# A mixture-of-experts layer on one core: slot rows and row fetches one stage later, the accumulator's writes issued from ScalarE, the residual joined in the last rounds

## The chip, the core and the metric

The kernel runs on one core of one Trainium2 chip. The metric is device time of one execution in microseconds. Three runs of the kernel before gave 2064.96, 2068.54 and 2069.97 us; the median, 2068.54, is the time to compare with. All engine names are those of the profile: PE is TensorE's matmul stream, PEld its weight loads, DVE is VectorE, ACT is ScalarE, POOL is GpSimd, SP is SyncE.

## The reference

One layer over 512 latent tokens of width 1024. A token mixer with two branches (a bidirectional RWKV scan and a gating MLP) comes first; the change does not touch it. Then comes this part, which it does touch:

```python
h = modulate(rmsnorm(x, norm2_g[l]), sh2, sc2)
x = x + ga2 * moe_ffn(h, lp)
...
return rmsnorm(x, final_norm_g)
```

`moe_ffn` sends every token to 4 of 32 experts. With `xblk` the rows of one expert's tokens, an expert computes

```python
gate = xblk @ lp['exp_w_gate'][e] + lp['exp_b_gate'][e]
up = xblk @ lp['exp_w_up'][e] + lp['exp_b_up'][e]
return clamped_swiglu(gate, up) @ lp['exp_w_down'][e] + lp['exp_b_down'][e]
```

and the results are added back to the tokens with softmax weights. All matrices are 1024 by 1024 in fp32, so the 32 experts read 96 of them, 4 MB each.

## The kernel before, in words

The part before the experts (projections, scan, merge, router) takes the first 834 us. The experts take the rest. They are written out by hand in `expert_chain` (from L1642): for PE, ACT and DVE the order of the program is the order of execution, while the DMA orders of SP and POOL are set by a scheduler.

**Rounds and places.** Round r has twelve places: 0 to 3 are the four weight blocks of the gate matrix of expert r, 4 to 7 the four blocks of the down matrix of expert r-1, 8 to 11 the four blocks of the up matrix of expert r. Round 0 has no down blocks, round 32 only down blocks. A weight block is 1 MB: SP loads it into a `raw` tile (six buffers), ACT casts it to fp32r (`wh`, L1481, called three blocks ahead), DVE forms the remainder (`wl`, L1487, two blocks ahead), and PE multiplies (L1498, L1499, L1503). A `raw` buffer is free again when the `wl` of its block is done.

**Between the blocks.** The activation of expert r-1 stands in round r: `up_clamp` and `up_half` on DVE at places 1 and 2, the transposes of `turn` on PE (L1583, followed by ACT's `aH`, L1586, and DVE's `aL`, L1587) after places 2 and 4. `x_rows` (L1534) lets POOL fetch the token rows of an expert by their slot numbers from DRAM; `x_turn` (L1547) transposes them after places 6 and 8. `y_out` scales an expert's output and lets POOL add it into the accumulator `d_acc` in DRAM.

**The side work.** `side` is a generator of which one piece is emitted per place, from round 0 on: `sum_start` forms the gate-weighted bias of the down projection on PE, copies it with ACT into a tile (L1425) and writes it to `d_acc` as the accumulator's start value (L1426 and L1429, five writes from SP, through one buffer, so that each pair of copies waits for the write before). Then `slot_rows` makes the slot numbers (L1379 to L1390) from a table that POOL scattered to DRAM and read back (`places`, L1368 and L1372), then `counts` (L1313 to L1322, with four small matmuls, L1318), `beyond` (L1438 to L1447) and `last_table` (L1752 to L1758).

**The end.** Experts 30 and 31 do not go through the accumulator: PE multiplies their outputs with a one-hot table. `x_load` and `sum_load`, emitted at the start of round 31, bring back the residual x, the final norm's weights, the gate `ga2` and the accumulator; `x_sum` (L1785, L1786) adds gate times accumulator to x on DVE, once for each of the four token tiles. `last_part(i, j)` (L1798, L1799) joins x of tile i and the expert output j in PSUM: j = 0 is expert 30, j = 1 is expert 31. The four tiles use PSUM tiles `gp`, `up`, `gp`, `up` in turn. `finish` then squares a tile on ACT (L1815), takes the root (L1816), scales on DVE (L1821), writes the output from SP (L1822), and copies the tile's sum back to x (L1823).

Of the kernel before, what the change touches and what calls it, by code (L numbers as in the profile page):

```python
# [154 lines left out]
class K:  # L155
# [1154 lines left out]
    def counts(self, pool):  # L1310
# [3 lines left out]
        pc = self.ps.tile([128, 32], F32, name="b1")  # L1314
# [9 lines left out]
    def places(self, pool):  # L1324
# [45 lines left out]
        self.tab = moe.tile([128, 4, NE, 2], F32, name="am")  # L1370
# [21 lines left out]
    def sum_start(self, pool):  # L1392
# [27 lines left out]
        for i in range(4):  # L1420
# [136 lines left out]
    def gate_sig(self, E):  # L1557
# [5 lines left out]
        nc.scalar.activation(sg, sg, AF.Sigmoid, scale=-1.702, bias=self.eps[:, 5:6])  # L1563

# [64 lines left out]
    def experts(self):  # L1629
        self.xf, self.xg, self.pss = [], {}, {}  # L1630
        self.nsplit = 0
# [15 lines left out]
    def expert_chain(self):  # L1647
# [31 lines left out]
        for i, (r, e, n, pos) in enumerate(seq):  # L1679
# [21 lines left out]
            elif pos == 4:  # L1701
                P["dn"] = ps.tile([128, 2, 512], F32, name="dn", bufs=1)
                if r == NE:
# [84 lines left out]
    def last_part(self, i, j):  # L1788

        nc = self.nc  # L1790
        if j == 0:
            self.pss[i] = self.ps.tile([128, 2, 512], F32, name=("gp", "up", "gp", "up")[i], bufs=1)
        ps = self.pss[i]
        y = self.ylast[j]
        for c in range(2):
            cs = slice(512 * c, 512 * c + 512)
            if j == 0:
                nc.tensor.matmul(ps[:, c, :], self.ident, self.xf[i][:, cs], start=True, stop=False)  # L1798
            nc.tensor.matmul(ps[:, c, :], self.wT[:, j, i, :], y[:, cs], start=False, stop=(j == 1))  # L1799

    def finish(self, P):

        nc = self.nc
        self.y_out(P)
        self.ylast[1] = P["y"]
        for i in range(4):
            if i > 1:
                self.last_part(i, 0)
            self.last_part(i, 1)
            x = self.xf[i]  # L1810
# [284 lines left out]
```

## Time and profile before

| what | value |
|---|---|
| median of three runs | 2068.54 us (2064.96 to 2069.97) |
| the profiled execution | 2063.39 us |
| its span, first to last instruction | 2061.6 us |
| PE busy | 1957.5 us (95%) |
| DVE busy | 1655.9 us (80%) |
| ACT busy | 1226.7 us (60%) |
| POOL busy | 422.9 us (21%) |
| mean granted clock of TensorE | 0.962 of full speed |

Busy shares are means over stages with different limits. Times on the timeline count from the span's start. In a timeline row the columns are start, duration, engine, line, operation, output and input, shape, how many, and in brackets the engine's idle time before the row with what ended it. A bracket that names an engine which had long been done hides another cause, often a DMA.

### The profile page before, as it was taken

What the parts mean: (1) busy time and instruction counts of PE and PEld (TensorE: products, weight loads), DVE (VectorE), ACT (ScalarE), POOL (GpSimd) and SP (SyncE); (2) the same over time, 40 slices, a digit from 0 to 9 for tenths busy, and PEclk for the clock granted to TensorE, in tenths of its full rate; (3) what the DMA queues carried; (4) which work ended last, traced back from release to release, by engine and by line L of the source; (5) the groups of instructions that cost most, each with busy time, mean ns of one, the idle gap of its engine ahead of it and who ended that gap; (6) DMA issues with size and microseconds to landing.
All of it is one profiled execution on the core that took longest, in us unless ns stands there. A gap on an engine that the chain in (4) does not pass through costs nothing.

```text
span 2061.6 us, 29221 instructions
## 1 busy us (share of the span) xinstructions
PE 1957.5 (95%) x11300; PEld 1524.1 (74%) x11300; DVE 1655.9 (80%) x1767; ACT 1226.7 (60%) x1387; POOL 422.9 (21%) x385
## 2 busy tenths in 40 slices
PE   7999889999999988889999999999999999999986
PEld 4667666666666678768888888888888888888863
DVE  5755875777766367789999999989999998999984
ACT  4522534343524244767777777777777777777752
POOL 0001605343423353510101011010101101010000
PEclk9999987988979998989999999999999999999999
DMA  8666232121112185789999999999999999999991
GB/s 312 212 204 196 61 118 78 40 64 32 51 42 69 33 270 215 278 288 377 364 373 368 371 369 367 375 364 379 369 371 368 365 374 367 375 366 374 366 357 43
DMA packets 153810, 534.26 MB, mean 259 GB/s; under 512 B 16160, under 2 KB 77344, under 8 KB 104513
## 3 DMA queue, kind: packets, MB, share of 16 engines
q1 hardware_dynamic: 141351, 500.57, 65.2%
q0 software_dynamic: 9952, 25.89, 5.2%
q10 hardware_dynamic: 2362, 5.87, 0.7%
q8 instruction: 91, 1.49, 0.3%
q14 instruction: 54, 0.44, 0.1%
HBM read 502.58 MB, written 37.65 MB: 262 GB/s over the span
## 4 chain that ended last, share of the span: by engine, by line
PE 72%; DVE 6%; issue 3%; POOL 3%; DMA 2%; ACT 1%; SPq 0%; POOLq 0%; DVEq 0%; ACTq 0%
PE dn L1499 6%; PE dn L1498 6%; PE dn L1503 6%; PE up L1498 6%; PE up L1499 6%; PE up L1503 6%; PE gp L1498 5%; PE gp L1499 5%; PE gp L1503 5%; PE fill L1082 4%; PE b L1583 1%; PE mm L868 1%; PE b L1547 1%; PE ch L909 1%; PE acc L165 1%
## 5 line engine op out<-in xcount | busy, mean ns | idle before, releaser
L1487 DVE TENSOR_TENSOR wl<-raw,wh 128x2048 fp32r<-128x2048 f32 x384 | 864.8, 2284 | 59.5 <-PE gp L1503 30.5
L1481 ACT CAST wh<-raw 128x2048 fp32r<-128x2048 f32 x384 | 721.5, 1905 | 104.9 <-PE gp L1499 68.3
L1498 PE MATMUL dn<-wh,aH 128*128 128x512 f32 x512 | 208.6, 407 | 6.5 <-ACT aH L1586 6.5
L1498 PE MATMUL gp<-wh,xH 128*128 128x512 f32 x512 | 206.4, 403 | 0.0
L1498 PE MATMUL up<-wh,xH 128*128 128x512 f32 x512 | 204.8, 400 | 0.0
L1499 PE MATMUL gp<-wh,xL 128*128 128x512 f32 x512 | 203.8, 398 | 0.0
L1499 PE MATMUL dn<-wh,aL 128*128 128x512 f32 x512 | 203.5, 397 | 0.0
L1534 POOL DMA_INDIRECT xg<-d_h,slots x30 | 33.9, 1129 | 824.4 <-PE b L1547 815.7
L1499 PE MATMUL up<-wh,xL 128*128 128x512 f32 x512 | 202.3, 395 | 0.0
L1503 PE MATMUL dn<-wl,aH 128*128 128x512 f32 x512 | 140.1, 395 | 0.0
L1503 PE MATMUL gp<-wl,xH 128*128 128x512 f32 x512 | 139.9, 395 | 0.0
L1503 PE MATMUL up<-wl,xH 128*128 128x512 f32 x512 | 139.3, 394 | 0.0
L1601 POOL DMA_INDIRECT d_acc<-y,slotd x30 | 105.0, 3501 | 132.4 <-ACT y L1600 99.7
L1586 ACT CAST aH<-b 128x512 fp32r<-128x512 f32 x64 | 37.6, 588 | 142.0 <-PE b L1583 142.0
L1498 PEld LDWEIGHTS dn<-wh,aH 128*128 128x128 f32 x512 | 97.1, 190 | 27.1 <-ACT aH L1586 7.0
L1503 PEld LDWEIGHTS gp<-wl,xH 128*128 128x128 f32 x512 | 96.6, 189 | 23.7
L1503 PEld LDWEIGHTS dn<-wl,aH 128*128 128x128 f32 x512 | 96.6, 189 | 22.3
L1499 PEld LDWEIGHTS gp<-wh,xL 128*128 128x128 f32 x512 | 97.0, 189 | 21.8
L1499 PEld LDWEIGHTS dn<-wh,aL 128*128 128x128 f32 x512 | 97.2, 190 | 21.3 <-DVE aL L1587 0.7
L1503 PEld LDWEIGHTS up<-wl,xH 128*128 128x128 f32 x512 | 96.1, 188 | 22.7
L1498 PEld LDWEIGHTS gp<-wh,xH 128*128 128x128 f32 x512 | 96.9, 189 | 21.6
L1498 PEld LDWEIGHTS up<-wh,xH 128*128 128x128 f32 x512 | 96.2, 188 | 22.2
(516 smaller groups left out, 3830.6 us busy)
## 6 DMA issues: line engine op xcount, KB each, us to landing
raw<-in_exp_w_gate_dram SPq DMA_DIRECT2D x128, 1024.0 KB, 7.0
raw<-in_exp_w_up_dram SPq DMA_DIRECT2D x128, 1024.0 KB, 9.2
raw<-in_exp_w_down_dram SPq DMA_DIRECT2D x128, 1024.0 KB, 7.1
raw<-in_w_ada_dram SPq DMA_DIRECT2D x32, 512.0 KB, 3.6
raw<-in_w_in_dram SPq DMA_DIRECT2D x24, 512.0 KB, 3.9
wa<-in_w_ada_dram SPq DMA_DIRECT2D x7, 1024.0 KB, 13.6
raw<-in_w_in_dram SPq DMA_DIRECT2D x6, 1024.0 KB
raw<-in_w_o_dram SPq DMA_DIRECT2D x8, 512.0 KB
```

What stands on the lines that cost most here:

```text
L165: return mm(ps, aH, bL, start=False, stop=last)
L868: nc.tensor.matmul(mm[:, par, d, :], BK[r, d, ch[d], :], AR[r, d, ch[d], :], start=True, stop=True)
L909: nc.tensor.matmul(sp[:, d, :], bk[:, d, :], uv[:, d, :], start=True, stop=True)
L1082: nc.tensor.matmul(ps, a[:, k, :], b[:, k, :], start=(n == 0), stop=(n == 23))
L1481: self.nc.scalar.copy(h, t)
L1487: self.nc.vector.tensor_sub(lo, t, h)
L1498: mm(ps[:, c, :], xH[:, k0 + kk, :], wh[:, cs], start=first and kk == 0, stop=False)
L1499: mm(ps[:, c, :], xL[:, k0 + kk, :], wh[:, cs], start=False, stop=False)
L1503: mm(ps[:, c, :], xH[:, k0 + kk, :], wl[:, cs], start=False, stop=last and kk == 1)
L1534: self.nc.gpsimd.indirect_dma_start(out=t, out_offset=None, in_=self.d_h2, in_offset=bass.IndirectOffsetOnAxis(ap=self.slots[:, e:e + 1], ...
L1586: nc.scalar.copy(aH, pt)
L1601: nc.gpsimd.indirect_dma_start(out=self.d_acc, out_offset=bass.IndirectOffsetOnAxis(ap=self.slotd[:, e:e + 1], axis=0), in_=y, in_offset=N ...
```

## The change

- **Round 1.** `counts` is split in two and comes right after `sum_start`. `slot_rows` waits until place 4 of round 1 is past (`rows_due`). The row fetches for experts 2 and 3 follow at places 4 and 5 instead of 3 and 5, and the transposes of expert 2's rows stand after places 8 and 10 instead of 6 and 8. The table read back from DRAM gets the buffer named `y` instead of `am`.
- **The accumulator's start value.** Its five writes are issued from ACT instead of SP.
- **The residual.** `x_sum(0)` stands at place 10 of round 31 instead of place 4; `x_sum` 1 to 3 stand at places 5 to 7 of round 32 (before: one at place 10 of round 31, two at places 6 and 7 of round 32).
- **The last four tiles.** Each has a PSUM tile of its own (`gp`, `up`, two `b1` tiles, `dn`). `last_part(1, 0)` moves from before the down blocks of expert 31 to behind them. The root's function table is asked for in round 31, behind the last sigmoid, and the four copies back to x stand at the very end, as eight halves.

```diff
+        yield
+        pc = self.ps.tile([128, 32], F32, name="b1")
         for j in range(4):
             nc.tensor.matmul(pc, self.ones, ch[:, j, :], start=(j == 0), stop=(j == 3))
...
-        self.tab = moe.tile([128, 4, NE, 2], F32, name="am")
+        self.tab = moe.tile([128, 4, NE, 2], F32, name="y")
...
-            nc.sync.dma_start(self.d_acc[128 * i:128 * i + 128, :], self.keep[:, 2048:3072])
+            nc.scalar.dma_start(self.d_acc[128 * i:128 * i + 128, :], self.keep[:, 2048:3072])
             yield
-        nc.sync.dma_start(self.d_acc[NLAT:NLAT + 128, :], self.keep[:, 2048:3072])
+        nc.scalar.dma_start(self.d_acc[NLAT:NLAT + 128, :], self.keep[:, 2048:3072])
...
+        if E["e"] == NE - 1:
+            nc.scalar.activation(self.moe.tile([128, 1], F32, name="rs", bufs=2), self.eps[:, 4:5], AF.Sqrt)
...
         yield from self.sum_start(self.small)
+        yield from self.counts(self.small)
+        yield
+        while not self.rows_due:
+            yield
         yield from self.slot_rows(self.small)
-        yield
-        self.counts(self.small)
         yield
         self.beyond(self.small)
...
-                    self.last_part(1, 0)
-                elif r == NE - 1:
-                    self.x_sum(0)
-            elif r == NE and pos > 5:
+            elif r == NE:
                 self.x_sum(pos - 4)
...
             elif pos == 10 and r == NE - 1:
-                self.x_sum(1)
+                self.x_sum(0)
...
-            elif pos in (6, 8) and r < NE and P:
-                self.x_turn(r + 1, pos // 2 - 3, xT)
+            elif pos in ((6, 8) if r > 1 else (8, 10)) and r < NE and P:
+                self.x_turn(r + 1, int(pos == (8 if r > 1 else 10)), xT)
+            if r == 1 and pos == 4:
+                self.rows_due = True
             next(side, None)
-            if r == 1 and pos in (3, 5):
-                self.x_rows(2 + (pos == 5))
+            if r == 1 and pos in (4, 5):
+                self.x_rows(pos - 2)
...
-            self.pss[i] = self.ps.tile([128, 2, 512], F32, name=("gp", "up", "gp", "up")[i], bufs=1)
+            if i < 3:
+                t = self.ps.tile([128, 2, 512], F32, name=("gp", "up", "dn")[i], bufs=1)
+                self.pss[i] = [t[:, 0, :], t[:, 1, :]], t.rearrange("p a b -> p (a b)")
+            else:
+                self.pss[i] = [self.ps.tile([128, 512], F32, name="b1") for _ in range(2)], None
...
+        self.last_part(1, 0)
         self.y_out(P)
         self.ylast[1] = P["y"]
-        for i in range(4):
-            if i > 1:
+        self.last_part(0, 1)
+        self.last_part(1, 1)
+        for n, i in enumerate((0, 1, 3, 2)):
+            if n > 1:
                 self.last_part(i, 0)
-            self.last_part(i, 1)
+                self.last_part(i, 1)
...
-            nc.scalar.copy(x, pf)
+        for i in (0, 1, 3, 2):
+            for c in range(2):
+                nc.scalar.copy(self.xf[i][:, 512 * c:512 * c + 512], self.pss[i][0][c])
```

The order on three engines follows. On DVE, the start of round 1, before: `slv` to `slots` are `slot_rows`, `sg` and the first `am` are the activation of expert 0.

```order
L1487 TENSOR_TENSOR wl<-raw,wh 128x2048 x2
L1379 TENSOR_REDUCE slv<-am 128x64
L1381 COPY wslot<-slv 128x32
L1383 TENSOR_SCALAR slm<-slv 128x32
L1385 SCALAR_TENSOR_TENSOR slots<-slm,slv 128x32
L1386 TENSOR_SCALAR slots<-slots 128x32
L1487 TENSOR_TENSOR wl<-raw,wh 128x2048
L1572 TENSOR_SCALAR sg<-up 128x1024
L1577 SCALAR_TENSOR_TENSOR am<-sg,gg 128x512
```

The same place in the changed kernel:

```order
L1315 TENSOR_SCALAR ch<-pm 128x128
L1488 TENSOR_TENSOR wl<-raw,wh 128x2048
L1576 TENSOR_SCALAR sg<-up 128x1024
L1581 SCALAR_TENSOR_TENSOR am<-sg,gg 128x512
L1321 TENSOR_REDUCE mc<-b_8532 128x1
L1323 CAST maxc<-mc 128x1
L1488 TENSOR_TENSOR wl<-raw,wh 128x2048
L1581 SCALAR_TENSOR_TENSOR am<-sg,gg 128x512
L1591 TENSOR_TENSOR aL<-b_8560,aH 128x512
L1488 TENSOR_TENSOR wl<-raw,wh 128x2048 x2
L1591 TENSOR_TENSOR aL<-b_8606,aH 128x512
L1380 TENSOR_REDUCE slv<-y 128x64
```

The slot rows moved from ahead of the activation to behind both of its halves and behind four more `wl`; the two steps of `counts` stand where they stood or close by.

On SP, rounds 0 and 1, before (`d_acc` are the accumulator's start writes):

```order
L1463 DMA raw<-in_exp_w_gate_dram 128x2048 x2
L1426 DMA d_acc<-mH 128x1024
L1463 DMA raw<-in_exp_w_gate_dram 128x2048
L1426 DMA d_acc<-mH 128x1024
L1463 DMA raw<-in_exp_w_gate_dram 128x2048
L1463 DMA raw<-in_exp_w_down_dram 128x2048
L1426 DMA d_acc<-mH 128x1024
L1463 DMA raw<-in_exp_w_down_dram 128x2048
L1426 DMA d_acc<-mH 128x1024
L1429 DMA d_acc<-mH 128x1024
L1463 DMA raw<-in_exp_w_down_dram 128x2048 x2
```

And now (the loads of `final_norm_g` and of `d_mod`, which is `ga2`, stood in round 31 before):

```order
L1464 DMA raw<-in_exp_w_gate_dram 128x2048 x4
L1464 DMA raw<-in_exp_w_down_dram 128x2048 x3
L1776 DMA mH<-in_final_norm_g_dram 128x1024
L1464 DMA raw<-in_exp_w_down_dram 128x2048
L1464 DMA raw<-in_exp_w_up_dram 128x2048
L1779 DMA mH<-d_mod 128x1024
L1464 DMA raw<-in_exp_w_up_dram 128x2048 x3
L1464 DMA raw<-in_exp_w_gate_dram 128x2048 x3
```

No weight load stands behind an accumulator write on SP any more, and two loads of 512 KB moved from round 31 to rounds 0 and 1.

On PE, the end of the program behind the last down block, before (`am` is the output of expert 31, `y` that of expert 30):

```order
L1799 MATMUL gp<-am,mH 128x512 x2
L1799 MATMUL up<-am,mH 128x512 x2
L1798 MATMUL gp<-xH,first 128x512
L1799 MATMUL gp<-y,mH 128x512
L1798 MATMUL gp<-xH,first 128x512
L1799 MATMUL gp<-y,mH 128x512
L1799 MATMUL gp<-am,mH 128x512 x2
```

And now:

```order
L1808 MATMUL up<-xL,first 128x512
L1809 MATMUL up<-y,mH 128x512
L1808 MATMUL up<-xL,first 128x512
L1809 MATMUL up<-y,mH 128x512
L1809 MATMUL gp<-am,mH 128x512 x2
L1809 MATMUL up<-am,mH 128x512 x2
L1808 MATMUL b_17150<-xL,first 128x512
L1809 MATMUL b_17150<-y,mH 128x512
```

The four matmuls of `last_part(1, 0)` now open this stretch, and the third tile goes to `b1` tiles instead of to `gp` again.

## Rows read from the trace of the kernel before

**Rows 1.** Stretches: round 1, then round 2 (busy, granted clock, DMA share, GB/s).
```profile
862.00:914.20 52.20, 39.28 (x171) 31.19 (x171) 38.82 (x43) 30.98 (x24) 12.99 (x9) 0.84 0.80 285
914.40:950.60 36.20, 36.20 (x166) 29.38 (x165) 33.77 (x21) 27.35 (x19) 4.62 (x3) 1.00 1.00 373
```

**Rows 2.** Timeline of PE in round 1: its two waits.
```profile
880.06 1.12 PE L1583 MATMUL b<-first,am 128*128 128x128 f32 x4 [9.46 <-DVE am L1577]
884.63 0.27 PE L1318 MATMUL b<-ch,ones 128*128 128x32 bf16 x4 [3.46 <-DVE ch L1316]
```

**Rows 3.** Timeline of DVE in round 1.
```profile
867.03 2.29 DVE L1487 TENSOR_TENSOR wl<-raw,wh 128x2048 fp32r<-128x2048 f32 x1 [4.50 <-ACT wh L1481]
874.22 0.58 DVE L1379 TENSOR_REDUCE slv<-am 128x64 f32<-128x256 f32 x1 [4.90 <-DMA am<-d_tab]
```

**Rows 4.** Timeline of ACT and its DMA issues, and of SP, rounds 0 and 1.
```profile
180.41 0.33 ACTq L552 DMA_DIRECT2D d_r<-ro  x1
...
848.02 0.33 SPq L1426 DMA_DIRECT2D d_acc<-mH  x1
...
851.09 1.08 ACT L1425 COPY mH<-b 128x512 f32<-128x512 f32 x2 [1.28 <-DMA d_acc<-mH]
...
858.43 0.33 SPq L1426 DMA_DIRECT2D d_acc<-mH  x1
...
864.12 1.07 ACT L1425 COPY mH<-b 128x512 f32<-128x512 f32 x2 [3.92 <-PE gp L1499]
```

**Rows 5.** DMA issues of the whole run: count, KB each, median us to landing.
```profile
d_acc<-mH SPq DMA_DIRECT2D x5, 512.0 KB, 3.8
...
d_v<-vo ACTq DMA_DIRECT2D x4, 384.0 KB, 4.8
...
d_r<-ro ACTq DMA_DIRECT2D x4, 256.0 KB, 2.0
...
d_acc<-y,slotd POOLq DMA_INDIRECT x30, 13.1
```

**Rows 6.** Waits of SP's queue, 830 to 900 us: total, times, longest.
```profile
SPq L1426 <- ACT mH L1425: 20.7, 4, 7.0
```

**Rows 7.** Timeline of POOL, round 1: the first row fetch.
```profile
876.34 2.37 POOL L1534 DMA_INDIRECT xg<-d_h,slots  x1 [8.33 <-DMA raw<-in_exp_w_down_dram]
```

**Rows 8.** Timeline of all engines in round 31, and the root's table load.
```profile
1965.82 0.49 SPq L1773 DMA_DIRECT2D mH<-d_mod  x1
...
1983.51 0.79 PE L1498 MATMUL dn<-wh,aH 128*128 128x512 f32 x1 [6.53 <-ACT aH L1586]
...
1988.95 1.22 DVE L1785 TENSOR_TENSOR raw<-raw,mH 128x1024 f32<-128x1024 f32 x1
...
1995.62 5.50 ACT L1481 CAST wh<-raw 128x2048 fp32r<-128x2048 f32 x3
1997.55 6.70 DVE L1487 TENSOR_TENSOR wl<-raw,wh 128x2048 fp32r<-128x2048 f32 x3
...
2037.89 1.28 ACT L1816 ACT_TABLE_LOAD   x1
```

**Rows 9.** Timeline of PE in round 32 and at the end.
```profile
2016.72 1.11 PE L1583 MATMUL b<-first,am 128*128 128x128 f32 x4 [3.52 <-DVE am L1577]
...
2021.79 0.79 PE L1498 MATMUL dn<-wh,aH 128*128 128x512 f32 x1
...
2034.74 1.98 PE L1799 MATMUL gp<-am,mH 128*128 128x512 f32 x4 [0.78 <-DVE am L1598]
...
2042.17 1.12 PE L1798 MATMUL gp<-xH,first 128*128 128x512 f32 x2 [3.74 <-ACT xH L1823]
```

**Rows 10.** Timeline of DVE in round 32.
```profile
2018.49 0.69 DVE L1587 TENSOR_TENSOR aL<-b,aH 128x512 fp32r<-128x512 f32 x1 [1.82 <-ACT aH L1586]
...
2026.23 0.69 DVE L1587 TENSOR_TENSOR aL<-b,aH 128x512 fp32r<-128x512 f32 x1 [6.07 <-ACT aH L1586]
...
2033.99 1.29 DVE L1598 TENSOR_TENSOR am<-dn,mH 128x512 f32<-128x512 f32 x2
```

More of the change, by code (lines that the diff above doesn't have):

```diff
@@ L1630, in experts @@
         self.xf, self.xg, self.pss = [], {}, {}
+        self.rows_due = False
         self.nsplit = 0
@@ L1796, in last_part @@
             cs = slice(512 * c, 512 * c + 512)
             if j == 0:
-                nc.tensor.matmul(ps[:, c, :], self.ident, self.xf[i][:, cs], start=True, stop=False)
-            nc.tensor.matmul(ps[:, c, :], self.wT[:, j, i, :], y[:, cs], start=False, stop=(j == 1))
+                nc.tensor.matmul(ps, self.ident, self.xf[i][:, cs], start=True, stop=False)
+            nc.tensor.matmul(ps, self.wT[:, j, i, :], y[:, cs], start=False, stop=(j == 1))
     def finish(self, P):
         nc = self.nc
+        self.last_part(1, 0)
@@ L1804, in finish @@
         self.y_out(P)
         self.ylast[1] = P["y"]
-        for i in range(4):
-            if i > 1:
+        self.last_part(0, 1)
+        self.last_part(1, 1)
+        for n, i in enumerate((0, 1, 3, 2)):
+            if n > 1:
                 self.last_part(i, 0)
-            self.last_part(i, 1)
-            x = self.xf[i]
+                self.last_part(i, 1)
+            parts, whole = self.pss[i]
             o = self.mbW.tile([128, 2048], F32, name="wh", bufs=4)[:, :1024]
-            pf = self.pss[i].rearrange("p a b -> p (a b)")
@@ L1813, in finish @@
             rs = self.moe.tile([128, 1], F32, name="rs", bufs=2)
-            ss = self.moe.tile([128, 1], F32, name="ss", bufs=2)
-            nc.scalar.activation(o, pf, AF.Square, accum_out=ss)
-            nc.scalar.activation(rs, ss, AF.Sqrt, bias=self.eps[:, 0:1], scale=1.0 / 1024)
-            nc.vector.reciprocal(rs, rs)
-            n = 1 + (i == 3)
-            for c in range(n):
-                cs = slice(1024 // n * c, 1024 // n * (c + 1))
-                nc.vector.scalar_tensor_tensor(o[:, cs], pf[:, cs], rs, self.fin[:, cs], op0=OP.mult, op1=OP.mult)
-                nc.sync.dma_start(self.out[128 * i:128 * i + 128, cs], o[:, cs])
@@ L1823, in finish @@
-            nc.scalar.copy(x, pf)
+            ss = self.moe.tile([128, 2], F32, name="ss", bufs=2)
+            if i < 3:
+                nc.scalar.activation(o, whole, AF.Square, accum_out=ss[:, 0:1])
+            else:
+                for c in range(2):
+                    nc.scalar.activation(o[:, 512 * c:512 * c + 512], parts[c], AF.Square, accum_out=ss[:, c:c + 1])
+                nc.vector.tensor_add(ss[:, 0:1], ss[:, 0:1], ss[:, 1:2])
+            nc.scalar.activation(rs, ss[:, 0:1], AF.Sqrt, bias=self.eps[:, 0:1], scale=1.0 / 1024)
@@ new lines, in finish @@
+            nc.vector.reciprocal(rs, rs)
+            for c in range(2):
+                cs = slice(512 * c, 512 * c + 512)
+                if n < 2:
+                    if c == 0:
+                        nc.vector.scalar_tensor_tensor(o, whole, rs, self.fin, op0=OP.mult, op1=OP.mult)
+                        nc.sync.dma_start(self.out[128 * i:128 * i + 128, :], o)
+                else:
+                    nc.vector.scalar_tensor_tensor(o[:, cs], parts[c], rs, self.fin[:, cs], op0=OP.mult, op1=OP.mult)
+                    nc.sync.dma_start(self.out[128 * i:128 * i + 128, cs], o[:, cs])
@@ L1825, in final_norm @@
+        for i in (0, 1, 3, 2):
+            for c in range(2):
+                nc.scalar.copy(self.xf[i][:, 512 * c:512 * c + 512], self.pss[i][0][c])
     def final_norm(self, i, pool, o, n=1):
```

3 lines of the change are left out of this document (1 added, 2 removed).

## The prediction

> **What bounds the kernel now.** I read the timeline by stretches first. In a steady round PE is busy for 36.20 of 36.20 us at full granted clock, with DVE at 33.77 us and the DMA engines at a share of 1.00 [rows 1]. So 29 of the 32 rounds belong to PE, DVE and DMA have little to spare, and the change touches nothing there. Round 1 is the exception: 52.20 us, of which PE works 39.28 at a mean clock of 0.84 and DVE 38.82 [rows 1]. Then I read who waits in it. PE stands still twice, 9.46 us for the activation of expert 0 and 3.46 us for the token counts, both from DVE [rows 2]. DVE stands still before that: 4.50 us for a cast of ACT, and 4.90 us at `slv` for the table that POOL reads back [rows 3]. DVE works in order, so the activation and three `wl` queue behind a table that PE does not need yet. At the other end two waits of PE matter: 6.53 us in round 31 for weights that come late [rows 8], and 3.74 us before the third token tile, whose PSUM tile ACT is still copying [rows 9].
>
> **Round 1: 7.7 us.** The slot rows move behind both halves of the activation and four `wl`. The table is read at 874.22 [rows 3]; behind the moved work (four `wl` of 2.29 us alone are 9.2 us) `slv` finds it ready, so that wait goes. What is late next is DVE itself: it has 38.82 us of work in 52.20 us [rows 1], thus 13.4 us of idle time. The first 4.50 us of it [rows 3] lie ahead of the slot rows and stay. The other 8.9 us follow from the slot rows or from PE's waits behind them, and go if DVE runs without a gap. PE needs less than that: its 39.28 busy us are partly at a low clock. So DVE, not PE, sets the length of the new round, and I expect short waits of PE for it at several places, the one-hot table of `last_table` among them.
>
> The new writes from ACT cost some of this, because the 4.50 us have a cause on ACT: it copies into one buffer and waits until each accumulator write has landed. The copy at 851.09 followed a write issued at 848.02, 3.1 us; the copy at 864.12 followed one issued at 858.43, 5.7 us [rows 4] (the bracket names PE, which was done long before). In the changed order ACT issues four of the five writes ahead of the cast that DVE waits for: 4 x 0.33 us by an earlier issue from ACT [rows 4], 1.3 us more. The landing of such a write from ACT is not in the trace. Its nearest rows are 3.8 us for these same writes from SP and 4.8 us for 384 KB from ACT [rows 5]; I take 4.3. The first wait then grows by 1.2 us and the last shrinks by 1.4, so DVE starts 1.1 to 1.2 us later: 8.9 - 1.2 = 7.7 us.
>
> Against this the Trainium skill's page "DMA: Bandwidth & Descriptors", section "Queues, rings and completion order", says that each DMA engine takes turns between the queues that have work, packet by packet. By that rule a write on ACT's own queue does not stand behind the megabytes of weights on SP's; with the lower row, 3.8 us, the first wait grows by 0.7, the last shrinks by 1.9, the round would gain 8.8 and the whole 12.7 us. No row here shows two busy queues with such a write, so I stay between the two rows.
>
> SP, freed of waiting 20.7 us for ACT's copies [rows 6], issues weight loads earlier; I give that no time of its own, since ACT did not wait for weights in this round. The two 512 KB loads that now stand in rounds 0 and 1 do not bind: 52.20 us at 285 GB/s are 14.9 MB, with 1.05 MB more 15.9 MB, which at the steady 373 GB/s [rows 1] take 42.7 us, below the 44.5 us that remain. The second of them waits on SP for the accumulator's last write; the weight loads behind it belong to places 9 to 11, and have some 10 us of slack. The split `counts` asks its matmuls one block earlier; what they then wait for is the same chain on DVE. The ends for the round: 13.4 us if all idle time of DVE goes, and less than nothing if the writes land late (below).
>
> **Round 31: 0.8 us.** The `ga2` load of 512 KB leaves SP's queue just ahead of the late weights [rows 8]. Alone on the engines it takes 1.4 us at 373 GB/s; beside the accumulator's read-back, which POOL issues at that time, up to twice that. I take 2.1 us off PE's wait of 6.53 us. But ACT now loads the root's table behind the sigmoid of this round: 1.28 us [rows 8], ahead of the three casts from 1995.62, and DVE's `wl` from 1997.55 starts the moment the first of these is done [rows 8]. From there DVE runs without a gap into PE's 3.52 us wait of round 32 [rows 9], so the load is paid: 2.1 - 1.3 = 0.8. Taking `x_sum(0)` out of place 4 frees 2.4 us of DVE (two operations of 1.22 [rows 8]) ahead of that point, where ACT is the later one, so I count nothing for it. Ends: -1.3 if the DMA gains nothing, 4 if the table load is covered and part of those 2.4 us counts.
>
> **Round 32 and the end: 3.1 us.** `last_part(1, 0)` leaves the stretch between PE's transposes, which end at 2017.83, and the down blocks, which start at 2021.79 [rows 9]: 3.96 us. The down blocks can now start when `aL` is done, at 2019.18 [rows 10], 2.6 us earlier, and end near 2031.4 instead of 2033.96. The second `aL` then ends at 2024.3 instead of 2026.92 [rows 10]; behind it come one `wl` (2.29) and now three `x_sum` (six operations of 1.22, 7.3 us, against 4.9 before), so DVE is free for `y` at 2033.9. Before, it took `y` at 2033.99 [rows 10]. So expert 31's output is neither earlier nor later; what moves in front of it is covered by `last_part(1, 0)`, which ends at 2031.4 + 3.96 = 2035.3, against a start of the next part at 2034.74 [rows 9]: 0.6 us lost. Behind that the same matmuls follow as before, without the wait of 3.74 us [rows 9], for the third and fourth tile have PSUM of their own. 3.74 - 0.6 = 3.1 us. The chain behind the last matmul is the same; the eight copies now at the end run beside the output's DMA. Ends: 0.5 us if a low clock after PE's wait eats the 2.6 us, 4 if `last_part(1, 0)` runs faster than it did there.
>
> **The sum.** 7.7 + 0.8 + 3.1 = 11.6 us. The profiled execution took 2063.39 us, so 2051.8 in its terms; it lies 5 us below the median of 2068.54, which is what the next times are to be held against: 2068.54 - 11.6 = 2056.9 us. About 0.3%, 6.2 us, is what a measurement of this kernel can tell from no change: faster means below 2062.3.
>
> **The rivals.**
> - *ACT becomes the bound, slower.* Each pair of copies waits in ACT's order for the write before, and every cast behind it waits too. POOL's scattered adds of the same size land after 13.1 us [rows 5]. If ACT's writes took that under full DMA load, the two waits seen would grow by 10.0 and 7.4 us, the covered one between by about as much: some 26 us, against 8.9 gained. 8.9 - 26 + 3.9 = -13, 2082 us. It decides from a landing of about 9 us on. Against it: the five writes took 3.8 us even in SP's queue [rows 5]. Chance 0.05.
> - *The row fetch comes late.* The slots are ready near 885 instead of 875.5, so the fetch, issued at 876.34 before [rows 7], goes out near 886, while PE reaches the transposes (two blocks later in order) near 895. If it lands like POOL's adds, after 13.1 us, PE waits 4 us, and the round gains 3.7: 2060.9. For it: POOL is slow and the DMA full; against it: a fetch only reads. Chance 0.14.
> - *The writes land quickly.* With the 2.0 us of a 256 KB write from ACT [rows 5], the waits shrink by 1.1 and 3.7 while the issues cost 1.3: DVE restarts 3.5 us earlier, the round gains 12.4, the whole 16.3: 2052.2. Against it: 373 GB/s would stretch the round to 42.7 us again, about 2055. Chance 0.15.
> - *The order does not do what it says,* and the slot rows still hold DVE: only 3.9 us remain, 2064.6. The order on DVE speaks against it. Chance 0.04.
>
> **The numbers.** The forecast has 0.62, with its own range 2051 to 2062 from the ends above taken two at a time. The range is 2049 to 2063: it leaves out the slower rival, the fourth, and the far end of the third. Faster: nearly all of the forecast, the third rival and most of the second, 0.85; same 0.10; slower 0.05.
>
> **What would show it.** In the changed profile round 1 lasts 44 to 45 us between the first blocks of rounds 1 and 2, `slv` follows `aL` without waiting for a DMA, and DVE has no idle time over 1 us from the third `wl` of the round on. ACT's waits for `d_acc` are 3 to 5 us each. PE's wait in round 31 is 4 to 5 us, its wait at the last activation 3.5 to 5. The last tiles follow each other on PE without a gap. A wait of ACT for a write above 9 us, or of PE for `xg`, would make the forecast wrong; so would a PE clock that falls in the new round 1 and stays low.

## The result, and the profile after

The changed kernel took 2057.17 us (median of nine runs, 2052.34 to 2061.63) against 2068.54 us for the kernel before, timed beside it (nine runs, 2063.47 to 2080.5). The ratio is 0.9942, with a 95% interval of 0.9920 to 0.9964: 11.4 us faster, with an interval of 7 to 17. Timed once more it took 2060.37 us against 2067.92, a ratio of 0.9966 (0.9945 to 0.9987), so 7.5 us. The forecast was 2056.9 us. The total held; two of its three terms did not, and by the means of two profiles each they erred in opposite directions.

The executions differ by more than the change is worth. In twelve of the thirteen profiles of this study the experts' first block began between 825.7 and 838.7 us, in one at 846.0, although nothing ahead of it was touched. I therefore cut each profile at rows that all of them have, PE's `gp<-bias,selE` at the start of rounds 0, 1, 2 and 31, and compare stretches. In the changed kernel the cuts are these, in the timeline of PE:

```profile
833.94 0.62 PE L1556 MATMUL gp<-bias,selE 128*128 128x512 f32 x2
...
867.28 0.62 PE L1556 MATMUL gp<-bias,selE 128*128 128x512 f32 x2
...
910.08 0.63 PE L1556 MATMUL gp<-bias,selE 128*128 128x512 f32 x2
...
1960.29 0.62 PE L1556 MATMUL gp<-bias,selE 128*128 128x512 f32 x2
```

Differences of such rows, and of the span's end, give the table (us). "To the turn" runs from round 31 to PE's transposes `b<-first,am` of round 32, "from the turn" from there to the span's end.

| kernel | rounds 0 and 1 | rounds 2 to 30 | to the turn | from the turn | sum |
|---|---|---|---|---|---|
| before | 27.21 + 53.61 = 80.8 | 1049.52 | 52.0 | 44.9 | 1227.2 |
| before, second profile (e5) | 27.13 + 53.68 = 80.8 | 1049.52 | 53.2 | 49.2 | 1232.7 |
| changed | 33.34 + 42.80 = 76.1 | 1050.21 | 52.5 | 42.4 | 1221.3 |
| changed, second profile (e11) | 33.15 + 45.32 = 78.5 | 1050.22 | 51.9 | 41.2 | 1221.8 |

By the means of two profiles each, the change gains 8.4 us: 3.5 in rounds 0 and 1, 0.4 to the turn, 5.2 from the turn, less 0.7 in the steady rounds. The first profiles alone give 5.9 us.

**Rounds 0 and 1.** The stretches of the changed kernel, in round 0, round 1 and round 2 (columns as in [rows 1]):

```profile
834.00:867.00 33.00, 27.95 (x112) 22.06 (x112) 22.14 (x15) 21.78 (x20) 22.67 (x18) 0.90 0.94 343
867.30:910.00 42.70, 38.44 (x177) 29.84 (x176) 38.15 (x42) 31.44 (x25) 9.32 (x4) 1.00 0.91 318
910.10:946.30 36.20, 36.20 (x165) 29.37 (x164) 34.39 (x21) 27.74 (x20) 4.51 (x2) 1.00 0.99 363
```

Round 1 is nearly 11 us shorter than before (53.61 to 42.80 us in the table), and PE's clock in it is full. But round 0 is 6.1 us longer. The timeline of PE shows the wait that is new there, and the short ones that are left in round 1:

```profile
861.47 1.28 PE L1424 MATMUL b<-mL 96*128 96x512 f32 x2 [5.05 <-ACT mH L1426]
...
878.04 0.66 PE L1587 MATMUL b<-first,am 128*128 128x128 f32 x4 [1.27 <-DVE am L1581]
...
898.85 0.63 PE L1548 MATMUL b<-first,xg 128*128 128x128 f32 x4 [1.77 <-DMA xg<-d_h,slots]
```

Before, PE waited 9.46 and 3.46 us in round 1 [rows 2], and 1.08 us for `b` in round 0. Behind the new wait PE runs at the low clock, as the granted clock (the third figure from the end of a row) of the stretch behind it, beside the next one, shows:

```profile
861.50:866.00 4.50, 4.50 (x11) 3.42 (x12) 1.71 (x1) 2.30 (x2) 2.08 (x4) 0.50 0.91 355
867.30:872.00 4.70, 4.70 (x22) 3.79 (x21) 1.14 (x1) 4.15 (x4) 0.00 (x0) 1.00 0.91 299
```

0.50 is the 1.2 GHz level, 1.00 the 2.4 GHz level. The cause of PE's wait is on ACT, whose timeline shows each pair of copies but the first waiting for the write that ACT issued before it:

```profile
847.56 0.33 ACTq L1427 DMA_DIRECT2D d_acc<-mH  x1
851.42 1.08 ACT L1426 COPY mH<-b 128x512 f32<-128x512 f32 x2 [1.53 <-DMA d_acc<-mH]
852.52 0.33 ACTq L1427 DMA_DIRECT2D d_acc<-mH  x1
...
860.83 1.07 ACT L1426 COPY mH<-b 128x512 f32<-128x512 f32 x2 [2.50 <-DMA d_acc<-mH]
861.93 0.33 ACTq L1427 DMA_DIRECT2D d_acc<-mH  x1
...
867.40 1.08 ACT L1426 COPY mH<-b 128x512 f32<-128x512 f32 x2 [3.14 <-DMA d_acc<-mH]
```

From the issue of a write to the next copy's start these are 3.9, 8.3 and 5.5 us. DVE pays for it, and then has the slot rows without a wait, as forecast:

```profile
864.29 2.29 DVE L1488 TENSOR_TENSOR wl<-raw,wh 128x2048 fp32r<-128x2048 f32 x1 [4.70 <-ACT wh L1482]
870.86 2.29 DVE L1488 TENSOR_TENSOR wl<-raw,wh 128x2048 fp32r<-128x2048 f32 x1 [4.28 <-ACT wh L1482]
...
887.01 0.62 DVE L1380 TENSOR_REDUCE slv<-y 128x64 f32<-128x256 f32 x1
```

**The end.** PE's waits in rounds 31 and 32 of the changed kernel, in its timeline, and the first rows of each of the last tile parts:

```profile
1976.31 0.79 PE L1499 MATMUL dn<-wh,aH 128*128 128x512 f32 x1 [3.78 <-ACT aH L1590]
...
1985.53 0.50 PE L1499 MATMUL dn<-wh,aH 128*128 128x512 f32 x1 [1.32 <-ACT aH L1590]
...
2006.28 1.10 PE L1808 MATMUL gp<-xH,first 128*128 128x512 f32 x2 [1.22 <-DVE xH L1792]
...
2012.82 0.66 PE L1587 MATMUL b<-first,am 128*128 128x128 f32 x4 [2.87 <-DVE am L1581]
...
2028.95 1.02 PE L1808 MATMUL up<-xL,first 128*128 128x512 f32 x2
...
2032.38 1.88 PE L1809 MATMUL gp<-am,mH 128*128 128x512 f32 x4
...
2035.81 1.02 PE L1808 MATMUL b<-xL,first 128*128 128x512 f32 x2
...
2040.96 1.02 PE L1808 MATMUL dn<-xH,first 128*128 128x512 f32 x2
...
2044.40 1.88 PE L1809 MATMUL dn<-am,mH 128*128 128x512 f32 x4
```

The wait of 6.53 us [rows 8] is 3.78 us, that of 3.52 us [rows 9] is 2.87, and the 3.74 us before the third tile [rows 9] are gone. The waits of 1.32 and 1.22 us are new, so that on the way to the turn little is gained: PE's waits there are 10.1 us in sum before and 9.4 us now. The last parts run from 2028.95 to 2046.28 without a gap, at full clock.

### The profile page after: what moved, and what is told of

It is laid out like the page before. It is cut to its first block, busy times and chain, and to the rows that moved or that the text cites. A ratio compares the mean times of both kernels' runs of the same rounds, so it can differ in the third digit from the quotient of the medians.

```text
span 2055.2 us, 29234 instructions
## 1 busy us (share of the span) xinstructions
PE 1955.0 (95%) x11300; PEld 1521.9 (74%) x11300; DVE 1654.9 (81%) x1769; ACT 1227.9 (60%) x1394; POOL 420.9 (20%) x385
## 5 line engine op out<-in xcount | busy, mean ns | idle before, releaser
L1500 PEld LDWEIGHTS up<-wh,xL 128*128 128x128 f32 x512 | 96.9, 189 | 22.0
```

Of the source, the lines that this page charges most:

```text
L1500: mm(ps[:, c, :], xL[:, k0 + kk, :], wh[:, cs], start=False, stop=False)
```

## The experiments

Nine variants, and each of the two kernels once more. The differences between them are a few us, which the medians hardly separate, so each is read by the stretches of its profile, one profile each. The stretches of the variants in one table:

| kernel | rounds 0 and 1 | rounds 2 to 30 | to the turn | from the turn | sum | median of runs |
|---|---|---|---|---|---|---|
| e1 two buffers | 27.30 + 42.46 = 69.8 | 1050.15 | 52.0 | 42.0 | 1213.9 | 2051.93 |
| e2 writes from SP | 27.12 + 45.20 = 72.3 | 1050.23 | 53.3 | 39.8 | 1215.7 | 2052.84 |
| e3 before, writes from ACT | 31.73 + 49.89 = 81.6 | 1049.53 | 51.7 | 47.8 | 1230.6 | 2068.12 |
| e4 before, rounds 0 and 1 | 33.19 + 43.92 = 77.1 | 1050.21 | 51.2 | 48.3 | 1226.8 | 2064.21 |
| e6 root's table late | 78.0 | 1050.22 | 50.7 | 39.8 | 1218.8 | 2055.95 |
| e7 `x_sum(0)` early | 76.5 | 1050.21 | 51.1 | 42.3 | 1220.1 | 2059.39 |
| e8 residual late | 77.2 | 1050.21 | 47.9 | 39.7 | 1215.0 | 2052.51 |
| e9 three joined | 69.8 | 1050.14 | 47.8 | 39.7 | 1207.5 | 2044.67 |
| e10 joined and `x_sum(0)` | 69.7 | 1050.15 | 46.1 | 41.8 | 1207.8 | 2046.00 |

### e1: two buffers for the start value

```diff
+            k0 = 2048 + 1024 * (i % 2)
-                o = self.keep[:, 2048 + 512 * c:2560 + 512 * c]
+                o = self.keep[:, k0 + 512 * c:k0 + 512 + 512 * c]
-            nc.scalar.dma_start(self.d_acc[...], self.keep[:, 2048:3072])
+            nc.scalar.dma_start(self.d_acc[...], self.keep[:, k0:k0 + 1024])
```

> The changed kernel, with the accumulator's start value formed in two buffers in turn instead of one. Theory A: what ate part of the gain in rounds 0 and 1 is the single buffer. ACT waited there 1.53, 2.50 and 3.14 us for writes that it had issued itself, PE 5.05 us behind it, and PE's clock fell. With two buffers a copy waits only for the write before the last: ACT's waits for d_acc fall under 0.5 us each, PE's wait for b under 1.5 us, and round 1 starts near 861 to 862 us instead of 867.3. DVE then sets round 1, so round 2 starts at 905 to 907 us instead of 910.1 and the time falls from 2057.2 to 2052 to 2054 us. Rival B: round 0's loss only moves a wait that round 1 has anyway (the table read back, the row fetch, DVE's work). Then round 1 starts early but PE's waits for am, xg and mH grow by the same 4 to 6 us, round 2 starts at 909 to 911 us, and the time stays within 1 us of 2057.

It took 2051.93 us, ratio to before 0.9923 (0.9897 to 0.9949). In its timeline of PE the wait in round 0 is back to its old size, at full clock, and round 1 starts 27.30 us after round 0:

```profile
857.07 0.99 PE L1425 MATMUL b<-mL 96*128 96x512 f32 x2 [1.19 <-ACT mH L1427]
860.69 0.62 PE L1557 MATMUL gp<-bias,selE 128*128 128x512 f32 x2
```

ACT has no wait for `d_acc` left. Rounds 0 and 1 are 6.4 us shorter than in the first profile of the changed kernel, round 1 as short as there (42.46 and 42.80 us), so nothing of it came back as a wait: theory A, a little better than its range. The single buffer cost the change 6.4 us in its first profile and 8.7 us in its second. What went is the wait and not the late landing: in e9, which has the same two buffers, such a write still landed up to 7.0 us after its issue.

### e2: the writes from SP again

```diff
-            nc.scalar.dma_start(self.d_acc[...], self.keep[:, 2048:3072])
+            nc.sync.dma_start(self.d_acc[...], self.keep[:, 2048:3072])
```

> The changed kernel, with the five writes of the start value issued from SP again. Theory A: the writes land late because they run beside weight loads that SP issues without a stop. From SP each write stands in the queue between the weights, and SP waits in between: landings go back to 3 to 5 us (from 3.9, 8.3 and 5.5 us on ACT), PE's wait for b in round 0 to about 1 us, round 1 starts near 861 to 862 us, round 2 at 904 to 907 us, and the time is 2052 to 2054 us. Rival B: the queue is not the cause but the load on the DMA engines; then the landing of the second write stays at 7 to 8 us and the time stays near 2057. Rival C: SP's waits for ACT's copies (20.7 us before the change) hold the weights back, ACT waits for raw tiles in round 1, and the time is 2058 to 2062 us.

It took 2052.84 us, ratio 0.9937 (0.9907 to 0.9967). Round 0 is at 27.12 us as A says: ACT's copy behind the second write, which waited 2.50 us in the changed kernel, does not wait any more. The wait that is left is ACT's last one, and SP waits again for ACT's copies. From the timeline of ACT and from the list of SP's waits:

```profile
868.90 1.08 ACT L1426 COPY mH<-b 128x512 f32<-128x512 f32 x2 [4.45 <-DMA d_acc<-mH]
```

```profile
SPq L1427 <- ACT mH L1426: 21.6, 4, 7.4
```

The write that this copy waited for went out from SP at 862.67 us, so it took 6.2 us, no less than the third write from ACT in the changed kernel (5.5 us). The median landings, 3.7 us here and 5.3 us there, do not weigh against that: they rest on two of the five writes here and three there, and leave out the second and the third in both.

Rounds 0 and 1 take 72.3 us, 4 to 6 us less than with writes from ACT through one buffer. So rival B (the load on the engines alone) is out for the second write, on which round 0 hangs, and C too: SP's 21.6 us of waiting cost nothing that shows in the sum. Theory A holds for round 0; round 1 is 2.7 us longer than in e1, behind the last copy.

The edit moved more than the writes. With them on SP, the scheduler asks for `final_norm_g` and `d_mod` in round 31 again, as before the change, and PE's wait before the down blocks has its old size again. From the timelines of SP and PE:

```profile
1951.71 0.44 SPq L1776 DMA_DIRECT2D mH<-in_final_norm_g_dram  x1
...
1962.34 0.51 SPq L1779 DMA_DIRECT2D mH<-d_mod  x1
```

```profile
1980.27 0.79 PE L1499 MATMUL dn<-wh,aH 128*128 128x512 f32 x1 [6.78 <-ACT aH L1590]
```

So the two loads move with the writes, and round 0 of e2 has 512 KB less to load. The issue from ACT was thus a loss in rounds 0 and 1, which a second buffer turns into a gain (69.8 us in e1), and what took the `d_mod` load out of round 31.

### e3: before, with the writes from ACT alone

```diff
-            nc.sync.dma_start(self.d_acc[...], self.keep[:, 2048:3072])
+            nc.scalar.dma_start(self.d_acc[...], self.keep[:, 2048:3072])
```

> The kernel before, with only the five writes issued from ACT. Theory A: the late landings come with this edit alone. Round 1 then starts 4 to 6 us later than before (866 to 868 instead of 861.6), but DVE waits for the table until about 874 us anyway, so only 0 to 2 us of that reach round 2 (915 to 918 us against 915.2), and the time is 2068 to 2071 us. Rival B: the late landings need the rest of the change too (other loads at that time); then round 1 starts at 861 to 863 us and the time is that of before or up to 2 us better. Rival C: the delay of round 0 adds to round 1 in full; 2073 to 2075 us.

2068.12 us, ratio 1.0003 (0.9979 to 1.0027). Round 0 grows by 4.5 us, round 1 shrinks by 3.7, since DVE waits for the table there in any case. Theory A. So the late landings come with this edit alone, and before the slot rows moved they were almost free. Two copies waited 4.68 and 4.70 us, each for a write issued 7.0 us earlier. The two loads move with this edit too, but they are not needed for a late write: the first was late before SP asked for `final_norm_g`, in the timelines of ACT and SP:

```profile
857.40 1.07 ACT L1425 COPY mH<-b 128x512 f32<-128x512 f32 x2 [4.68 <-DMA d_acc<-mH]
```

```profile
863.63 0.38 SPq L1770 DMA_DIRECT2D mH<-in_final_norm_g_dram  x1
```

### e4: before, with the edits of rounds 0 and 1 alone

```diff
         yield from self.sum_start(self.small)
+        yield from self.counts(self.small)
+        yield
+        while not self.rows_due:
+            yield
         yield from self.slot_rows(self.small)
...
-            nc.sync.dma_start(self.d_acc[...], self.keep[:, 2048:3072])
+            nc.scalar.dma_start(self.d_acc[...], self.keep[:, 2048:3072])
```

> The kernel before with the edits of rounds 0 and 1 alone (slot rows, counts, row fetches and transposes moved, table in the buffer y, writes from ACT); the residual, the last parts and the four tiles at the end stay as before. Theory A: the gains of the two ends of the kernel are independent. Round 2 then starts at 909 to 911 us as in the changed kernel, PE's wait of 3.74 us before the third tile is there again, and the time is 2.5 to 3.5 us above that of the changed kernel: 2059.5 to 2061. Rival B: what is gained in round 1 is lost later, because the DMA engines are full in the steady rounds and the weights then come late: the start of the last block row moves by less than 3 us, and the time is 2063 to 2066 us.

2064.21 us, ratio 0.9985 (0.9966 to 1.0003). Rounds 0 and 1 take 77.1 us as in the changed kernel, and the steady rounds give nothing back, so B's mechanism is not there although the time lies in B's range. It lies there because the old end is dearer than A had it: 48.3 us from the turn against 42.4 and 41.2. The timeline of PE behind the 3.7 us wait shows why:

```profile
2040.83 2.08 PE L1804 MATMUL gp<-xH,first 128*128 128x512 f32 x2 [3.73 <-ACT xH L1829]
2042.70 1.91 PE L1805 MATMUL gp<-y,mH 128*128 128x512 f32 x2
2044.41 1.92 PE L1804 MATMUL gp<-xH,first 128*128 128x512 f32 x2
```

In the first profile of before the first of these pairs took 1.12 us [rows 9], and the second, in its timeline of PE:

```profile
2043.13 1.02 PE L1799 MATMUL gp<-y,mH 128*128 128x512 f32 x2
```

### e5: the kernel before once more

No edit.

> The kernel before, unchanged, profiled once more. In the one profile of before the stretch from round 31 to the end took 96.87 us, in two kernels with the same end (only the writes from ACT; rounds 0 and 1 alone) 99.5 and 99.4 us, with PE at the low clock behind its waits where the first profile had the high one. Theory A: the first profile of before was lucky there, and its 2063.39 us is low against the median of 2067 to 2068.5 for that reason: now the stretch takes 98.5 to 100 us, with low-clock rows (1.9 us for two matmuls) at the last parts. Rival B: the difference belongs to the hoisted loads in those two kernels; then the stretch takes 96.5 to 97.5 us again, and what before has above its first profile lies in the phase ahead of the experts, whose start moved between 833.4 and 838.7 us in the profiles so far.

One profile, 2064.02 us. From round 31 on it took 102.4 us, even more than A said. The granted clock of the stretch behind PE's wait of 3.74 us, in this profile:

```profile
2039.60:2045.00 5.40, 5.36 (x7) 2.26 (x8) 1.45 (x2) 2.31 (x4) 0.00 (x0) 0.50 0.45 178
```

and the same stretch in the first profile of before:

```profile
2042.10:2047.00 4.90, 4.83 (x12) 2.20 (x13) 1.45 (x2) 2.34 (x5) 0.00 (x0) 1.00 0.47 186
```

The same wait, 3.74 us in both, was followed once by the low level and once by the high one. The four profiles with the old end (before, e5, e3, e4) have 44.9, 49.2, 47.8 and 48.3 us from the turn, so the one on which I built the forecast is the most favourable of them. That the stretch ahead of the experts differs is true as well: this profile began the experts 4.9 us earlier, which is why its time is still 2064.

### e6: the root's table in finish

```diff
-        if E["e"] == NE - 1:
-            nc.scalar.activation(self.moe.tile([128, 1], F32, name="rs", bufs=2), self.eps[:, 4:5], AF.Sqrt)
...
     def finish(self, P):
         nc = self.nc
+        nc.scalar.activation(self.moe.tile([128, 1], F32, name="rs", bufs=2), self.eps[:, 4:5], AF.Sqrt)
         self.last_part(1, 0)
```

> The changed kernel, with the root's function table asked for at the start of finish instead of behind the last sigmoid. Theory A (the step of the prediction): the table load of 1.28 us and its 0.20 us operation stand on the chain of ACT's casts and DVE's wl, where DVE now stands idle for 1.90 us; at the new place ACT is idle for 12.96 us anyway. The stretch from round 31 to the end gets 1.3 to 1.9 us shorter (94.9 to 93.0 to 93.6 us). Rival B: late weights or PE bound that stretch, the load is covered, and it changes by less than 0.5 us.

2055.95 us, ratio 0.9958 (0.9936 to 0.9980), by its ratio no different from the changed kernel. By the profile, DVE's wait in front of the three `wl` of round 31 in the changed kernel is

```profile
1993.64 6.70 DVE L1488 TENSOR_TENSOR wl<-raw,wh 128x2048 fp32r<-128x2048 f32 x3 [1.90 <-ACT wh L1482]
```

and here, with ACT's table load at its new place:

```profile
1987.71 6.70 DVE L1488 TENSOR_TENSOR wl<-raw,wh 128x2048 fp32r<-128x2048 f32 x3 [0.57 <-ACT wh L1482]
...
2012.85 1.28 ACT L1811 ACT_TABLE_LOAD   x1
```

1.33 us less, and the way to the turn is 1.2 to 1.8 us shorter: theory A, and the size that the prediction gave this step. The rest of the gain in the table (39.8 us from the turn) is the clock: PE waited only 1.44 us before the turn here, and stayed at the high level (granted 1.00 from 2003.3 to 2030 us). e2, e8 and e9, with waits of 0.9 to 1.3 us there, have 39.7 or 39.8 us as well.

### e7: x_sum(0) back at place 4 of round 31

```diff
+                elif r == NE - 1:
+                    self.x_sum(0)
             elif r == NE:
                 self.x_sum(pos - 4)
...
             elif pos == 10 and r == NE - 1:
-                self.x_sum(0)
                 self.ylast = {0: P["y"]}
```

> The changed kernel, with x_sum(0) back at place 4 of round 31, where it was before. Theory A: the prediction was wrong to count its move at nothing. At place 4 DVE stood idle for 3.66 us, while at place 10 the two operations of 1.22 us lie on DVE's unbroken chain from 1993.64 to PE's wait of 2.87 us in round 32, so the stretch from round 31 to the end gets 2 to 2.5 us shorter (94.9 to about 92.5 us) and PE's wait of 1.22 us for xH goes. Rival B: the accumulator's read-back, which needed 15.3 us to land (till about 1980), or ACT's casts bound that stretch as well, so that DVE only waits elsewhere: less than 0.7 us.

2059.39 us, ratio 0.9961 (0.9941 to 0.9981). The way to the turn is 0.8 to 1.4 us shorter, between the two theories: DVE is rid of 2.4 us there, but then waits 1.36 us for a cast of weights that are not there yet. And PE's wait before the turn is now 4.57 us, after which it runs at the low clock (42.3 us from the turn). Inconclusive by the time, and no reason to put it back.

### e8: the last residual tiles at place 8

```diff
                     self.x_load(0)
-                    self.x_load(1)
                     self.sum_load()
...
+            if r == NE - 1 and pos == 8:
+                self.x_load(1)
             w = lo.pop(i)
```

> The changed kernel, with the last two tiles of the residual asked for at place 8 of round 31 instead of place 0, so that SP issues them behind the weights. Theory A: PE's wait of 3.78 us in round 31 (6.53 before) comes from SP standing before these loads until a tile of round 30 is free (1960.5), while the DMA engines ran down to 14 GB/s. Without that the weights are asked for earlier, PE's wait falls to 0 to 1 us, the clock stays, and the stretch from round 31 to the end gets 2 to 4 us shorter. Rival B: the engines are full with the accumulator's 2 MB from 1964.7 on, and the wait falls by 1 us at most. Rival C: the wait goes, but DVE and ACT, the bound of rounds 31 and 32, give it back at PE's wait for the last activation (2.87 us), which grows by as much.

2052.51 us, ratio 0.9941 (0.9910 to 0.9971). PE's wait of 3.78 us before the down blocks of round 31 is gone. What PE waits for in rounds 31 and 32 now (the list of waits: total, times, longest):

```profile
PE gp L1809 <- DVE xH L1793: 5.1, 1, 5.1
PE b L1587 <- DVE am L1581: 0.9, 1, 0.9
```

To the turn it takes 47.9 us against 52.5 and 51.9: 4 to 4.6 us less. Theory A in size; C in part, since DVE is what PE waits for now. SP's queue shows the cause. In the changed kernel it gets to the two residual tiles when round 31 has begun (1960.29), and to the weights 1.1 us after that beginning:

```profile
1960.48 0.32 SPq L1771 DMA_DIRECT2D xH<-d_xn  x1
1960.85 0.48 SPq L1771 DMA_DIRECT2D xL<-d_xn  x1
1961.43 5.02 SPq L1464 DMA_DIRECT2D raw<-in_exp_w_down_dram  x4
```

and here 2.4 us before round 31 begins (1962.30), with no residual in front of them:

```profile
1959.86 8.60 SPq L1464 DMA_DIRECT2D raw<-in_exp_w_down_dram  x4
```

### e9: two buffers, late table and late residual together

The edits of e1, e6 and e8.

> The changed kernel with three edits together: two buffers for the start value, the root's table asked for in finish, the last two residual tiles at place 8 of round 31. Theory A: they act on stretches that do not touch, so their gains add. Measured from the first block of the experts to the span's end: 27.3 us for round 0, 42.5 for round 1, 1050.2 for rounds 2 to 30, and from round 31 on 87.6 us (the late residual alone) less 1.4 us (the table): 1206 us against 1221.3 us of the changed kernel and 1213.9 us with two buffers alone. The time is 12 to 16 us below that of the changed kernel run beside it. Rival B: with the earlier edits the end is already bound by DVE, and the third edit only moves waits: 1209 to 1212 us.

2044.67 us against 2060.37 for the changed kernel timed beside it; ratios to before 0.9891 (0.9857 to 0.9926) and 0.9966. The sum of stretches is 1207.5 us, 14 us below the changed kernel: theory A within 1.5 us, except that the late table adds nothing to the late residual (47.8 and 47.9 us to the turn). It beats both kernels of this case.

### e10: the same, and x_sum(0) at place 5

```diff
             elif pos == (5 if P else 9) and E:
                 self.gate_sig(E)
+                if r == NE - 1:
+                    self.x_sum(0)
...
             elif pos == 10 and r == NE - 1:
-                self.x_sum(0)
                 self.ylast = {0: P["y"]}
...
+            nc.sync.dma_start(self.fin, bcast_rows(self.A["final_norm_g"]))
+            nc.sync.dma_start(self.ga2, bcast_rows(self.d_mod[3]))
```

The last two lines ask for `ga2` together with the first residual tiles.

> The kernel with those three edits, and x_sum(0) at place 5 of round 31 (the gate ga2 is asked for with the first residual tiles for it). Theory A: DVE stood idle there for 2.52 us with the late residual, waiting for a cast of weights that came late, so that the two operations of 1.22 us leave DVE's chain into the last activation: 1.5 to 2.4 us less than the kernel with three edits, 1204 us. Rival B: the accumulator's read-back lands after 14 us, near 14 us into round 31 plus 4, when DVE reaches place 5: DVE waits for it and the next wl come later; no gain or up to 2 us lost.

2046.00 us, ratio 0.9902 (0.9869 to 0.9936), the same as e9 within the intervals. The way to the turn is 1.7 us shorter, as A said, and the way from it 2.0 us longer, which neither theory had. In the timeline of PE:

```profile
1991.73 1.12 PE L1585 MATMUL b<-first,am 128*128 128x128 f32 x4 [7.19 <-DVE am L1579]
...
1993.52 0.79 PE L1500 MATMUL dn<-wh,aH 128*128 128x512 f32 x1 [0.68 <-ACT aH L1588]
```

PE's idle time before the turn now lies in one wait of 7.19 us, and the clock is low behind it; in e9 nearly the same time is split into 5.75 and 0.96 us around `last_part(0, 0)`, and the down blocks run at full clock (0.50 for the same row).

### e11: the changed kernel once more

No edit.

> The changed kernel once more, beside the two above. From the first block of the experts to the span's end it should take 1219 to 1224 us again (1221.3 us in its first profile), with ACT's waits for the accumulator's writes and PE's wait of about 5 us in round 0. The stretch from round 31 on should take 92.5 to 96 us, against 96.9 and 102.4 us in the two profiles of before: the spread of 5.5 us that before has there came from the low clock behind PE's waits at the very end, which the changed kernel does not have. If it has the spread too, that reading is wrong.

2060.37 us, ratio 0.9966 (0.9945 to 0.9987). 1221.8 us from the first block of the experts, 93.1 us from round 31 on: as expected. PE's wait in round 0 is here two of 2.69 and 2.53 us, because another one of the writes landed late (ACT waited 5.31 us for the first).

## Why the prediction was right, and where it was not

**Round 1.** What was said of DVE held. The slot rows find the table ready, the 4.90 us of [rows 3] and PE's 9.46 and 3.46 us are gone, and the round lasts 42.8 to 45.3 us against 44 to 45 forecast. The forecast took the 52.20 us of [rows 1] for the whole round; from first block to first block it was 53.61 us, so that its own gain would have given 45.9 us.

**The step that failed** is the price of ACT's waits: "The first wait then grows by 1.2 us and the last shrinks by 1.4, so DVE starts 1.1 to 1.2 us later". I took a landing of 4.3 us for every write. From the issue to the copy that waited for it, the first three writes took 3.9, 8.3 and 5.5 us in the first profile and 7.7, 6.5 and 5.8 us in the second. The 3.8 us of [rows 5], from which I had started, is a median over two of its five writes. The wait in between, which I counted as covered, was not, and PE stood for it in round 0. DVE's last late `wl` moved from 867.03 to 870.86 us, and the experts had begun 0.45 us earlier: 4.3 us where the forecast had 1.2. Put into the same sum, 8.9 - 4.3 = 4.6 us, which is what the first pair of profiles gives for rounds 0 and 1 (80.82 - 76.14 = 4.7; the second pair gives 2.3). e1 confirms it from the other side: without these waits the gain is 11.1 us. The rival "ACT becomes the bound" had this mechanism, with 13.1 us for a write; it came in part.

The Trainium skill's page "DMA: Bandwidth & Descriptors", section "Queues, rings and completion order", says that each DMA engine takes turns, packet by packet, between the queues that have work. I had concluded that a write on ACT's queue does not stand behind SP's weights, and had turned this into 3.8 us per write and 12.7 us in all. The trace does not bear that conclusion out. For the late write of the changed kernel, issued at 852.52 us, these are the queues' packets, megabytes and shares of the DMA engines from 852.5 to 856 us and from 856 to 860.5 us (q1 has SP's transfers, q10 ACT's writes; before the change, with the writes on SP, q10 has no packet from 840 to 870 us):

```profile
q1 hardware_dynamic: 159, 1.17, 98.2%
```

```profile
q1 hardware_dynamic: 194, 1.37, 72.9%
q10 hardware_dynamic: 144, 0.52, 28.5%
```

In the first 3.5 us not one packet of the write ran, while SP's queue kept the engines full; then the two queues shared them for 4.5 us. The second stretch agrees with turns between the queues; why the write began so late no run shows. In e1, too, the second write had no packet for 3.8 us.

**Round 31.** The two sizes held: PE's wait fell by 2.2 us on average (6.53 and 6.25 us to 3.78 and 4.50), and the table load costs 1.3 us (e6). Other runs bear out the first: the wait is 3.73 us in e3 and 4.65 in e4, where the loads of `ga2` and `final_norm_g` have left that stretch and no other edit touches it, and 6.78 us in e2, where both are back. Net, PE's waits up to the turn are 10.1 and 10.4 us in the two profiles before and 9.4 us in both after, which agrees with 0.8 us; the stretch itself differs by 1.2 us between the two profiles of before. What I did not see is what else made these weights late: the residual loads in front of them, worth 4 us and more (e8).

**The end.** The 3.1 us came out as 2.5 in the profile on which they were built, and were too few by the means. The wait of 3.74 us went, `last_part(1, 0)` moved at no visible loss, and from the turn on the change gains 5.2 us by the means of two profiles, because behind that wait PE mostly ran at the low clock: the three pairs behind it in e4 took 5.9 us instead of 3.2. My single profile was the exception, and I priced the wait by its length alone.

**The sum.** 8.4 us by stretches and 7.5 to 11.4 us by the runs, where 11.6 was forecast. That the median came out 0.3 us from the forecast is partly luck.

**The signs.** `slv` follows `aL` without a wait for a DMA, DVE stands idle for at most 0.3 us at a time behind 870.86, and the last tiles follow each other without a gap, as the prediction said. ACT's waits for `d_acc`, 3 to 5 us each by the prediction, were 1.53, 2.50 and 3.14 us, and 5.31, 0.72 and 3.42 us in e11, since the work between a write and the next copy covers part of the landing. PE's wait at the last activation, 3.5 to 5 us by the prediction, was 2.87 and 2.88 us. One of the signs of being wrong came: PE waited for `xg`, 1.77 us and in e11 0.65 us. That is the rival of the late row fetch at less than half of its 4 us, beside the 5 us that PE lost in round 0.

**Left open.** The steady rounds are 0.02 us longer each (36.21 against 36.19 us), 0.7 us in all, in every kernel with the moved slot rows (1050.14 to 1050.23 against 1049.52) and in none without. No run was made to find out why.

## What to carry to other kernels

When a transfer moves to another engine's queue, the engine that reuses its buffer inherits the landing time: give it a second buffer before counting the freed queue as a gain. Price a wait of TensorE by its length and by the rows behind it, since these may run at half clock, and take a second profile before trusting the one that shows them fast. On a queue in order, look at what stands in front of late weights: a load that waits for a buffer holds up all that stands behind it.

## What the hardware showed that I had not expected

- After the same wait of 3.74 us PE was granted 0.50 of full speed in one execution of a kernel and 1.00 in another. Before the turn, waits of 0.9 to 1.4 us (e2, e6, e8, e9) were followed by rows at the high level; behind those of 2.87 us and more, rows at the low level followed in every profile. This is no rule of lengths: in round 31 of the changed kernel the low level (0.50 from 1986.5 to 1989.7) followed a wait of 1.32 us.
- 512 KB writes from ACT beside the weight loads landed after 3.1 to 8.3 us where the traces resolve it (3.8 to 6.1 in the changed kernel, 4.3 to 7.6 in its second profile, 3.1 to 6.9 in e3, 4.4 to 8.3 in e7), and which of them was late changed from one execution to the next. The second write of the changed kernel, 8.3 us from its issue to the copy that waited, is not among the resolved ones; for its first 3.5 us it had no packet on the engines.
- The same code ahead of the experts took between 825.7 and 846.0 us, with the granted clock from 400 to 600 us between 0.85 and 0.91 in the thirteen profiles.
